# Splitting the later modulation products between GpSimd and ScalarE in a one-core transformer block

## The chip, the cores and the metric

The kernel runs on one core of a Trainium2 chip. The time of an execution is device time in microseconds from its first to its last instruction, with what lies around it. The core has five instruction queues that run side by side and meet through semaphores: TensorE (PE, matmuls; PEld is its loading of weights), VectorE (DVE), ScalarE (ACT), GpSimd (POOL) and SyncE (SP, which here only issues DMAs). Each queue executes strictly in the order in which its instructions were written.

## What is computed

A transformer block on 256 tokens of width 2048, in float32: modulation from a conditioning vector c, one wide projection, a gated delta net (GDN) beside a sparse attention (NSA), a mixing and output projection, and a mixture of 16384 small experts (PEER).

```python
    cs = jax.nn.silu(c)
    for l in range(DEPTH):
        mod = cs @ ada_w[l] + ada_b[l]
        sh1, sc1, g1, sh2, sc2, g2 = [m[:, None, :] for m in jnp.split(mod, 6, axis=-1)]
        h = _rmsnorm(x, norm1_w[l]) * (1.0 + sc1) + sh1
        (a_q, a_k, a_v, a_z, a_a, a_b, b_q, b_kc, b_vc, b_ks, b_vs, b_kw, b_vw, b_g,
         m_a, m_b) = jnp.split(h @ w_in[l], offsets, axis=-1)
        o_a = _gated_deltanet(a_q, a_k, a_v, a_z, a_a, a_b, gdn_conv_w[l], gdn_A_log[l],
                              gdn_dt_bias[l], gdn_norm_w[l])
        o_b = _nsa(b_q, b_kc, b_vc, b_ks, b_vs, b_kw, b_vw, b_g, positions,
                   cmp_pos_k[l], cmp_w1_k[l], cmp_w2_k[l], cmp_pos_v[l], cmp_w1_v[l], cmp_w2_v[l])
        y = jax.nn.sigmoid(m_a) * (o_a @ w_branch_gdn[l]) + jax.nn.sigmoid(m_b) * (o_b @ w_branch_nsa[l])
        x = x + g1 * (y @ w_out[l])
        h2 = _rmsnorm(x, norm2_w[l]) * (1.0 + sc2) + sh2
        x = x + g2 * _peer(h2, peer_wq[l], peer_keys1[l], peer_keys2[l], peer_u[l], peer_v[l])
    return _rmsnorm(x, final_norm_w)
```

The first two parts of the modulation (sh1, sc1) are needed at once. The change is about the next three, g1, sh2 and sc2: 3 x 2048 sums of 2048 products with c, needed only when `w_out` is done.

## The kernel before

**Weights.** Every dense weight passes through one stream (`Stream`). SyncE loads raw tiles of 128x1024 (512 KB, `raw`), into four slots after the first stage. Each half is split into a high part by ScalarE (`whi`, `S.copy`) and the rest by VectorE (`wlo`, raw minus whi); five such pairs can lie ready (`NSPL = 5`). TensorE makes six matmuls of 128x512 from one pair. A raw slot is loaded anew when the pair's `wlo` is done.

**Stages.** Up to about 205 us the first projections run with the modulation's first parts; then the rest of the wide projection with the GDN heads beside it (tiles qkv, cv, kb, vb, XY, N, o); then attention (P, PT, obh); then the two branch projections (`wn`, in four units of 16 weight slices, each ended by `sb<-ps,sb` and `sb<-sa,sb` on VectorE) and `wo` (again four units, each ended by `x<-ps,g1b`, `x<-x,xr`, a square with a row sum on ScalarE and a store `x1d<-x` by GpSimd). From about 1045 us on the experts run to the end.

**Background work.** Dense units are written out one after the other. Between their matmuls a planner (`Background`, with a table of costs in `Times`) steps small tasks whose times have come, so the order of all queues is settled when the program is built. When its clock has advanced by `PACE` (4.5) or, after the last GDN head, `PACE2` (3.3), it also takes one step of `ada_gen`.

**Later modulation.** `ada_gen` is `ada_late((G1, SH2, SC2), ...)`. A step takes one 128x512 tile of the weights (`adas`, two buffers, loaded by SyncE from `ada_t`), multiplies it by a copy of c (`crow`) and sums each row into one column of `acol`, all in one VectorE instruction (SCALAR_TENSOR_TENSOR and its read of the accumulator). Then it issues the load of the tile after next into the slot that has come free. 64 steps make one part; the sums go to `mcol`, and g1 also through `adarow` to `modr`, from where it is loaded as `g1b`. A second use of `ada_late`, for g2 in the experts' stage, has its own tiles.

**The keys' tiles.** `kv_rot` (for kc, ks and kw) and `vcvs_task` (for vc) copy projected keys and values from PSUM to `kv_t`, two tiles a call from one pool of three buffers. Keys are rotated on VectorE, then all are transposed by TensorE.

**GpSimd's queue** in this part of the program holds clears (`o`, `PTc`) and DMA issues: `mix<-partd` and `mix<-mixd` (partial results that a dense unit will use), `sa`, `sb`, `g1b`, `xr` and the stores `x1d`.

Of the kernel before, what the change touches and what calls it, by code (L numbers as in the profile page):

```python
# [7 lines left out]
F32 = mybir.dt.float32  # L8
# [4 lines left out]
AF = mybir.ActivationFunctionType  # L13
OP = mybir.AluOpType
# [145 lines left out]
def flat(ap, off, *dims):  # L160
    return bass.AP(tensor=ap.tensor, offset=ap.offset + off, ap=[list(x) for x in dims])
# [229 lines left out]
def build(nc, tc, A, out, dump=None, stop=None):  # L391

    dump = dump or (lambda n, a: None)

    def at(name):
        if stop == name:
            raise Stop()

    stacks = []
    with ExitStack() as top:  # L400
        top.enter_context(tc.manual_schedule())
        try:
            _build(nc, tc, A, out, stacks, dump, at, stop)
        except Stop:
            pass
        for s in reversed(stacks):
            s.close()


def _build(nc, tc, A, out, stacks, dump, at, stop_at):  # L410
    times = Times()
    V, S, G, PE, SP = (Timed(e, n, times) for e, n in (
        (nc.vector, "V"), (nc.scalar, "S"), (nc.gpsimd, "G"), (nc.tensor, "P"), (nc.sync, "Q")))
# [5 lines left out]
    def pool(st, name, bufs=1, space=None, side=None):  # L419
        kw = {}  # L420
        if space is not None:
            kw["space"] = space
        if side is not None:
            kw["side"] = side
        return TimedPool(st.enter_context(tc.tile_pool(name=name, bufs=bufs, reuse_waits="tile", **kw)), name, bufs, times)
# [7 lines left out]
    def ps():  # L433
        return pss.tile([128, 512], F32, name="ps")

    def act(out, in_, func, bias=0.0, scale=1.0, **kw):
        return S.activation(out, in_, func, bias=bias, scale=scale, **kw)
# [10 lines left out]
    def wait_for(what):  # L448
        while what not in done:
            yield  # L450
# [196 lines left out]
    sbp = pool(st_a, "adasb", side=LEFT)  # L647
    n2T = sbp.tile([128, KT], F32, name="n2T")
    crow = sbp.tile([128, D], F32, name="crow")
# [65 lines left out]
                          start=True, stop=True)  # L715
            V.tensor_copy(dst[:, k4 * 512:(k4 + 1) * 512], p)

    def ada_late(parts, crow, acol, row, room):

        raws = []  # L720
        n = 64 * len(parts)

        def load():
            m = len(raws)
            r = room(m)
            SP.dma_start(r, flat(A["ada_t"], (64 * (parts[m // 64] - 2) + m % 64) * 128 * 512, (512, 128), (1, 512)))
            raws.append(r)

        for _ in range(2):
            load()  # L730
        yield
        for i, part in enumerate(parts):
            for m in range(64):
                r = raws[64 * i + m]
                q = m % 4
                V.scalar_tensor_tensor(r, r, 1.0, crow(q), op0=OP.mult, op1=OP.mult,
                                       accum_out=acol[:, m // 4, q:q + 1])
                if len(raws) < n:
                    load()
                yield  # L740
            col = mcol[:, part, :]
            V.tensor_reduce(col, acol, axis=AX.X, op=OP.add)
            V.tensor_tensor(col, col, adabT[:, 16 * part:16 * part + 16], OP.add)
            if part == SC2:
                V.scalar_tensor_tensor(col, col, 1.0, n2T, op0=OP.add, op1=OP.mult)
            if part in (G1, G2):
                yield bg.now() + 4.0
                p = ps()
                PE.transpose(p[:16, 0:128], col, ident)
                S.copy(row, p[:16, 0:128])  # L750
                G.dma_start(flat(modr, D if part == G2 else 0, (128, 16), (1, 128)), row)
            done.add(part)
            yield

    ada_gen = ada_late((G1, SH2, SC2), lambda q: crow[:, 512 * q:512 * q + 512], sbp.tile([128, 16, 4], F32, name="acol"),
                       sbp.tile([16, 128], F32, name="adarow"),
                       lambda m: sbp.tile([128, 512], F32, name="adas", bufs=2))

    def ada_until(*parts):

# [124 lines left out]
    rp = pool(st_f, "rp", side=LEFT)  # L885
# [124 lines left out]
    def rope(dst, src, tb, n):  # L1010

        t1 = rp.tile([128, n, 32], F32, name="rt1", bufs=2)
        b = lambda a, s: a[:, tb, None, s].to_broadcast([128, n, 16])
        lo, hi = slice(0, 16), slice(16, 32)
        V.tensor_tensor(t1[:, :, lo], src[:, :, hi], b(rs, lo), OP.mult)
        V.tensor_tensor(t1[:, :, hi], src[:, :, lo], b(rs, hi), OP.mult)
        V.tensor_tensor(dst[:, :, 0:32], src[:, :, 0:32], rc[:, tb, None, :].to_broadcast([128, n, 32]), OP.mult)
        V.tensor_tensor(dst[:, :, 0:32], dst[:, :, 0:32], t1, OP.add)

    def transpose_to(p, src, n):  # L1020
        for i in range(n):
            PE.transpose(p[:, i * 128:(i + 1) * 128], src[:, i, :], ident)
        return p[:, :n * 128].rearrange("p (n t) -> p n t", n=n)

    def kv_rot(a, o, dst, free):

        rts = []
        for tb in range(2):
            r = rp.tile([128, 2, 128], F32, name="kv_t", bufs=3)
            S.copy(r, a[tb][:, o:o + 256].rearrange("p (g d) -> p g d", g=2))  # L1030
            rts.append(r)
        banks.give(free)
        yield from wait_for("rope")
        yield
        for tb in range(2):
            rope(rts[tb], rts[tb], tb, 2)
        yield
        yield from banks.take()
        p = ps()
        for tb in range(2):  # L1040
            transpose_to(p[:, tb * 256:(tb + 1) * 256], rts[tb], 2)
        yield
        V.tensor_copy(dst.rearrange("p g (b t) -> p b g t", b=2), p.rearrange("p (b g t) -> p b g t", b=2, g=2))
        banks.give()
# [224 lines left out]
    def kc_task():  # L1269
        yield from kv_rot(c0, 64, kcT[:, 0], 1)  # L1270
        done.add("kc")
# [7 lines left out]
    def vcvs_task(a):  # L1279
        vt = []  # L1280
        for tb in range(2):
            r = rp.tile([128, 2, 128], F32, name="kv_t", bufs=3)
            S.copy(r, a[tb][:, 0:256].rearrange("p (g d) -> p g d", g=2))
            V.tensor_copy(vsw[:, tb, 0], a[tb][:, 256:512].rearrange("p (g d) -> p g d", g=2))
            vt.append(r)
        banks.give(2)
        yield
        p = ps()
        for tb in range(2):
            transpose_to(p[:, tb * 256:(tb + 1) * 256], vt[tb], 2)  # L1290
        S.copy(kcT[:, 1].rearrange("p g (b t) -> p b g t", b=2), p.rearrange("p (b g t) -> p b g t", b=2, g=2))
        yield from wait_for("kc")
        yield
        windows(0)
        yield
        windows(1)
        done.add("vc")

    def kskw_task(a):
        for w in range(2):  # L1300
            yield from kv_rot(a, 256 * w, kT[:, :, w, :], 2 * w)
        done.add("k")
# [58 lines left out]
    def windows(i):  # L1361
        lq, w = i // 2, i % 2
        for g in range(2):
            s = kcT[:, w, g, :]
            win = bass.AP(tensor=s.tensor, offset=s.offset + 4 * lq, ap=[list(s.ap[0]), [1, 4], [16, 15]])
            V.tensor_tensor(blocks[i % 3][:, :, g, 0:15], win,
                            cpos[:, w, 4 * lq:4 * lq + 4, None].to_broadcast([128, 4, 15]), OP.add)
# [45 lines left out]
    cmp_gen = cmp_task()  # L1413

    kv_tasks = dict(vcvs=vcvs_task, kskw=kskw_task, vw=vw_task)
    for n in ORDER:
        if n[0] == "m":
# [515 lines left out]
    def g2_task():  # L1933

        crow = [last_load(vp_(), flat(crowd, 1024 * i, (0, 128), (1, 1024))) for i in range(2)]
        room, small = vp_(), vp_()
        x1_load(0)
        start = bg.now()
        for m, v in enumerate(ada_late((G2,), lambda q: crow[q // 2][:, q % 2 * 512:q % 2 * 512 + 512],
                                       small[:, 0:64].rearrange("p (n q) -> p n q", q=4), small[0:16, 128:256],  # L1940
                                       lambda m: room[:, m % 2 * 512:m % 2 * 512 + 512])):
            yield -max(start + G2PACE * m, bg.now() + 2.0, v or 0.0)
        for half in range(2):
            g2b.append(last_load(vp_(), flat(modr, D + 1024 * half, (0, 128), (1, 1024))))
        x1_load(1)
        for half in range(2):
            fwb.append(last_load(vp_(), flat(A["fnw"], 1024 * half, (0, 128), (1, 1024))))
        done.add("last")
# [124 lines left out]
```

## Time and profile before

| | us |
|---|---|
| median of 3 runs | 2617.65 (2614.93 to 2621.04) |
| the profiled execution | 2625.61 |
| its span, first to last instruction | 2623.8 |
| busy: PE, DVE, ACT, POOL | 2561.7, 1873.9, 1416.3, 521.1 |
| later modulation, first to last product | 224.2 to 1036.3 |

Busy shares are averages over the whole span; what an edit in one stage is worth is read from the waits of that stage. All kernel lines appear as L293, the helper that records every operation, so groups are told apart by their tiles. `ps` is a PSUM tile, `ht` one of the activations' tiles.

### The profile page before, as it was taken

Reading aid. Unit: us, or ns where it says so; the run is one execution under the profiler, and the core shown is the slowest. Engines: PE = TensorE matmul, PEld = TensorE weight load, DVE = VectorE, ACT = ScalarE, POOL = GpSimd, SP = SyncE. Lnnn points to the kernel's source line nnn. Section 1 sums busy time; section 2 is a strip of 40 time slices with the busy share of each in tenths; the row PEclk is TensorE's granted clock in tenths of the full one; section 3 lists DMA queues with packets and bytes.
Section 4 is the critical chain, followed back from the end, with each engine's and each line's share of the span. In section 5 each row is a group of like instructions: output and inputs, shape, how many; then the busy total and the mean of one; then the engine's idle time right before and its main releaser. Section 6 shows DMA issues by size and latency. Waiting matters only on the chain.

```text
span 2623.8 us, 42855 instructions
## 1 busy us (share of the span) xinstructions
PE 2561.7 (98%) x14774; PEld 2122.5 (81%) x14774; DVE 1873.9 (71%) x4089; ACT 1416.3 (54%) x2901; POOL 521.1 (20%) x467
## 2 busy tenths in 40 slices
PE   7999999999999999999999999999999999999998
PEld 5777777686877777999998888888778888888886
DVE  5666877776778776889885555555588887766666
ACT  3435756655555444555555555555555555655555
POOL 0001000000000000016666666662011112000000
PEclk9999999999999999999999999999999999999999
DMA  8887866667676887456666776776588888555554
GB/s 329 333 306 271 277 220 222 236 239 254 216 253 225 287 289 260 179 179 184 183 183 186 189 185 185 189 186 200 212 297 292 288 292 295 189 187 191 185 190 155
DMA packets 229130, 604.60 MB, mean 230 GB/s; under 512 B 59984, under 2 KB 60320, under 8 KB 228400
## 3 DMA queue, kind: packets, MB, share of 16 engines
q1 hardware_dynamic: 168336, 538.21, 58.7%
q0 software_dynamic: 49632, 40.58, 8.9%
q10 hardware_dynamic: 10944, 23.07, 2.3%
q8 instruction: 116, 1.90, 0.3%
q14 instruction: 102, 0.84, 0.1%
HBM read 571.72 MB, written 30.04 MB: 229 GB/s over the span
## 4 chain that ended last, share of the span: by engine, by line
PE 85%; DVE 6%; DMA 4%; ACT 3%; issue 1%; ACTq 0%; DVEq 0%; SPq 0%; POOLq 0%
PE ps L293 85%; DVE wlo L293 2%; DMA adas<-ada_t 2%; DMA raw<-w_in 1%; ACT whi L293 1%; DMA ht<-ada_t 1%; DVE adas L293 1%; DVE cv L293 1%; ACT L293 0%; ACT o L293 0%; DVE A L293 0%; DVE ht L293 0%; DMA ccom<-consts 0%; ACT gsq L293 0%; DVE big L293 0%
## 5 line engine op out<-in xcount | busy, mean ns | idle before, releaser
L293 DVE TENSOR_TENSOR wlo<-raw,whi 128x512 fp32r<-128x512 f32 (+2 forms) x1632 | 1099.6, 685 | 526.0 <-ACT whi L293 494.7
L293 ACT CAST whi<-raw 128x512 fp32r<-128x512 f32 (+2 forms) x1632 | 997.3, 617 | 770.3 <-PE ps L293 615.7
L293 PE MATMUL ps<-ht,whi 128*128 128x256 f32 (+1 forms) x3152 | 817.6, 335 | 0.8 <-DVE ht L293 0.8
L293 PE MATMUL ps<-ht,wlo 128*128 128x256 f32 x2304 | 648.5, 281 | 0.3
L293 PEld LDWEIGHTS ps<-ht,whi 128*128 128x128 f32 x3152 | 533.5, 188 | 68.7 <-DVE ht L293 1.0
L293 PE MATMUL ps<-whi,ht 128*128 128x512 f32 (+2 forms) x1536 | 522.4, 402 | 8.2 <-ACT whi L293 4.0
L1851 POOL DMA_INDIRECT gated<-gate,place x256 | 416.1, 1625 | 294.8 <-DMA gated<-gate,place 177.0
L293 PEld LDWEIGHTS ps<-ht,wlo 128*128 128x128 f32 x2304 | 434.2, 188 | 1.0 <-DVE wlo L293 0.9
L293 PE MATMUL ps<-wlo,wh 128*128 128x512 f32 x1024 | 407.2, 398 | 4.1 <-DVE wlo L293 4.1
L293 PE MATMUL ps<-whi,wl 128*128 128x512 f32 x1024 | 406.7, 397 | 0.0
L293 PE MATMUL ps<-whi,wh 128*128 128x512 f32 x1024 | 403.8, 394 | 2.0 <-ACT wh L293 2.0
L293 PEld LDWEIGHTS ps<-whi,ht 128*128 128x128 f32 x1536 | 289.5, 190 | 92.1 <-issue 12.4
L293 PE MATMUL ps<-wlo,ht 128*128 128x512 f32 (+2 forms) x768 | 300.8, 392 | 6.3 <-DVE wlo L293 6.1
L293 PEld LDWEIGHTS ps<-wlo,wh 128*128 128x128 f32 x1024 | 193.0, 189 | 52.9 <-DVE wlo L293 5.4
L293 PEld LDWEIGHTS ps<-whi,wh 128*128 128x128 f32 x1024 | 192.8, 188 | 50.3 <-ACT wh L293 2.3
L293 PEld LDWEIGHTS ps<-whi,wl 128*128 128x128 f32 x1024 | 193.1, 189 | 45.2 <-DVE wl L293 0.2
L293 ACT CAST wh<-A 128x256 fp32r<-128x256 f32 x256 | 103.9, 407 | 135.8 <-PE ps L293 130.3
L293 PEld LDWEIGHTS ps<-wlo,ht 128*128 128x128 f32 x768 | 146.5, 191 | 35.0 <-DVE wlo L293 10.8
L293 DVE SCALAR_TENSOR_TENSOR adas<-adas,crow 128x512 f32<-128x512 f32 x192 | 131.4, 685 | 36.7 <-DMA adas<-ada_t 36.3
L293 DVE TENSOR_TENSOR wl<-A,wh 128x256 fp32r<-128x256 f32 x256 | 108.7, 425 | 48.8 <-ACT wh L293 48.1
L293 POOL DMA_DIRECT2D gates<-gated x128 | 68.4, 539 | 353.5 <-DVE A L293 340.7
L293 ACT COPY aj<-ps 128x256 f32<-128x256 f32 x91 | 33.9, 373 | 78.6 <-PE ps L293 78.6
(319 smaller groups left out, 2204.6 us busy)
## 6 DMA issues: line engine op xcount, KB each, us to landing
raw<-u SPq DMA_DIRECT2D x256, 512.0 KB, 3.6
raw<-v SPq DMA_DIRECT2D x256, 512.0 KB, 4.2
raw<-w_in SPq DMA_DIRECT2D x170, 512.0 KB, 4.9
adas<-ada_t SPq DMA_DIRECT2D x192, 256.0 KB, 3.7
raw<-ada_w SPq DMA_DIRECT2D x64, 512.0 KB, 6.7
gated<-zero ACTq DMA_DIRECT2D x64, 256.0 KB, 4.1
raw<-wn SPq DMA_DIRECT2D x32, 512.0 KB, 4.7
raw<-wo SPq DMA_DIRECT2D x32, 512.0 KB, 5.0
```

Source lines behind the costliest of these rows:

```text
L293: r = f(*args, **kw)
L1851: nc.gpsimd.indirect_dma_start(gated[tb].rearrange("i j (t o) -> (i j t) o", o=1), bass.IndirectOffsetOnAxis(ap=place[:, tb, n:n + 1], axi ...
```

## The change

`ada_late` gets a parameter, `pool`. Where it is set, as for `ada_gen`, a step is two instructions: GpSimd multiplies the tile by c in place, and ScalarE copies the tile onto itself with a row sum into `acol`. The loads, the two `adas` buffers and the pace stay. The pool of `kv_t` gets a fourth buffer. The use for g2 is not changed.

```diff
@@ -715,7 +715,7 @@
-    def ada_late(parts, crow, acol, row, room):
+    def ada_late(parts, crow, acol, row, room, pool=False):
@@ -733,8 +733,12 @@
                 r = raws[64 * i + m]
                 q = m % 4
-                V.scalar_tensor_tensor(r, r, 1.0, crow(q), op0=OP.mult, op1=OP.mult,
-                                       accum_out=acol[:, m // 4, q:q + 1])
+                if pool:
+                    G.tensor_tensor(r, r, crow(q), OP.mult)
+                    act(r, r, AF.Copy, accum_out=acol[:, m // 4, q:q + 1])
+                else:
+                    V.scalar_tensor_tensor(r, r, 1.0, crow(q), op0=OP.mult, op1=OP.mult,
+                                           accum_out=acol[:, m // 4, q:q + 1])
                 if len(raws) < n:
                     load()
                 yield
@@ -754,7 +758,7 @@
-                       lambda m: sbp.tile([128, 512], F32, name="adas", bufs=2))
+                       lambda m: sbp.tile([128, 512], F32, name="adas", bufs=2), True)
@@ -1026,7 +1030,7 @@
-            r = rp.tile([128, 2, 128], F32, name="kv_t", bufs=3)
+            r = rp.tile([128, 2, 128], F32, name="kv_t", bufs=4)
@@ -1279,7 +1283,7 @@
-            r = rp.tile([128, 2, 128], F32, name="kv_t", bufs=3)
+            r = rp.tile([128, 2, 128], F32, name="kv_t", bufs=4)
```

Since the planner counts GpSimd's and ScalarE's time otherwise than VectorE's, the whole order after about 205 us is laid anew. Two places show what stands where.

ScalarE at the second unit of `wn`, around the first cast to `yh` (the transposed result of the first unit), in the kernel before:

```order
L293 CAST whi_9666<-raw_9553 128x512
L293 CAST whi_9679<-raw_9553 128x512
L293 CAST whi_9691<-raw_9578 128x512
L293 CAST yh_9643<-ps_9698 128x4x128
L293 CAST whi_9716<-raw_9578 128x512
L293 CAST yh_9643<-ps_9708 128x4x128
```

and now:

```order
L293 CAST whi_9831<-raw_9719 128x512
L293 ACTIVATE adas_9748,acol_107<-adas_9748 128x512
L293 CAST whi_9845<-raw_9719 128x512
L293 CAST whi_9857<-raw_9741 128x512
L293 CAST whi_9867<-raw_9741 128x512
L293 ACTIVATE adas_9777,acol_107<-adas_9777 128x512
L293 CAST whi_9883<-raw_9767 128x512
L293 ACTIVATE adas_9843,acol_107<-adas_9843 128x512
L293 CAST yh_9808<-ps_9890 128x4x128
```

A row sum of adas stands between the casts to whi, after every one to three of them, and each waits for its product on GpSimd.

GpSimd where the branch projections' inputs are loaded (`sa`, `sb`, two buffers each), in the kernel before:

```order
L293 DMA mix_9075<-mixd_2200 128x1024
L293 DMA sa_9648<-mixd_2200 128x1024
L293 DMA sb_9649<-mixd_2200 128x1024
L293 DMA sa_9652<-mixd_2200 128x1024
L293 DMA sb_9653<-mixd_2200 128x1024
L293 DMA sa_9660<-mixd_2200 128x1024
L293 DMA sb_9661<-mixd_2200 128x1024
```

and now:

```order
L293 TENSOR_TENSOR adas_9713<-adas_9713,crow_96 128x512
L293 DMA sa_9813<-mixd_2200 128x1024
L293 DMA sb_9814<-mixd_2200 128x1024
L293 DMA sa_9817<-mixd_2200 128x1024
L293 DMA sb_9818<-mixd_2200 128x1024
L293 DMA sa_9825<-mixd_2200 128x1024
L293 DMA sb_9826<-mixd_2200 128x1024
L293 TENSOR_TENSOR adas_9748<-adas_9748,crow_96 128x512
L293 TENSOR_TENSOR adas_9777<-adas_9777,crow_96 128x512
```

The products of adas stand behind loads that wait for a buffer (the third `sa` for the first one's use), here and at the loads of mix and the stores of x1d.

## Rows read from the trace of the kernel before

**Rows 1.** The page's head: span, and each engine's busy time.

```profile
span 2623.8 us, 42855 instructions
PE 2561.7 (98%) x14774; PEld 2122.5 (81%) x14774; DVE 1873.9 (71%) x4089; ACT 1416.3 (54%) x2901; POOL 521.1 (20%) x467
```

**Rows 2.** The tile adas: duration (min/median/max, ns), first and last start; landing.

```profile
L293 DVE SCALAR_TENSOR_TENSOR adas<-adas,crow x192: 669/684/694, 224.2 to 1036.3; 128x512 f32<-128x512 f32 x192
...
DMA to landing us min/median/max: 2.4/3.7/8.9
```

**Rows 3.** Stretches (us from the start): each engine's busy time, clock, DMA.

```profile
core 0: us, PE busy (x) PEld busy (x) DVE busy (x) ACT busy (x) POOL busy (x), PEclk, DMA share, GB/s
205.00:300.00 95.00, 92.71 (x485) 72.33 (x484) 69.14 (x187) 64.67 (x142) 7.76 (x23) 1.00 0.79 271
205.00:1045.00 840.00, 811.50 (x4802) 637.96 (x4801) 629.34 (x1641) 473.52 (x1107) 24.41 (x57) 0.99 0.73 250
```

**Rows 4.** TensorE's waits, 205 to 1045 us: total, times, longest.

```profile
PE ps L293 <- DVE wlo L293: 11.6, 17, 3.4
PE ps L293 <- ACT whi L293: 3.1, 4, 1.3
PE ps L293 <- DVE XY L293: 2.4, 2, 1.8
PE ps L293 <- ACT N L293: 2.2, 2, 2.0
PE ps L293 <- DVE cv L293: 2.2, 2, 1.6
PE ps L293 <- DVE mix L293: 2.1, 3, 1.2
```

**Rows 5.** VectorE's waits, 205 to 1045 us: the one for adas.

```profile
DVE adas L293 <- DMA adas<-ada_t: 36.3, 20, 5.0
```

**Rows 6.** Five stretches around VectorE's longest waits for adas: the first, the sum.

```profile
604.90:614.30 9.40, 6.00 (x26) 4.50 (x24) 4.14 (x10) 3.00 (x5) 0.00 (x0) 0.93 0.83 290
...
sum 44.00, PE 35.72 PEld 27.13 DVE 20.93 ACT 17.99 POOL 0.18; mean PE 7.14 PEld 5.43 DVE 4.19 ACT 3.60 POOL 0.04
```

**Rows 7.** Groups by form, 205 to 1045 us: busy us, mean ns | idle before.

```profile
L293 DVE TENSOR_TENSOR wlo<-raw,whi 128x512 fp32r<-128x512 f32 x427 | 285.6, 688 | 128.4 <-ACT whi L293 125.3
L293 ACT CAST whi<-raw 128x512 fp32r<-128x512 f32 x426 | 257.5, 623 | 227.2 <-PE ps L293 164.1 <-DMA raw<-w_in 20.0 <-DVE mx L293 14.3
...
L293 DVE SCALAR_TENSOR_TENSOR adas<-adas,crow 128x512 f32<-128x512 f32 x192 | 131.4, 685 | 36.7 <-DMA adas<-ada_t 36.3
...
L293 DVE DVE_READ_ACCUMULATOR adas<-adas,crow 128x1 f32 x192 | 15.7, 82 | 0.0
```

**Rows 8.** The same view: ScalarE's square with a row sum, and its read.

```profile
L293 ACT ACTIVATE ps<-x 128x512 f32<-128x512 f32 x6 | 3.6, 602 | 11.5 <-DVE x L293 11.5
...
L293 ACT ACTIVATION_READ_ACCUMULATOR ps<-x 128x1 f32 x6 | 1.1, 187 | 0.0
```

**Rows 9.** ScalarE's waits: whi from 205 to 1045 us, kv_t before 300 us.

```profile
ACT whi L293 <- PE ps L293: 168.0, 207, 4.8
...
ACT kv_t L293 <- PE ps L293: 3.0, 1, 3.0
```

**Rows 10.** SyncE's own waits, 205 to 1045 us.

```profile
SPq L293 <- DVE adas L293: 316.1, 180, 6.1
```

**Rows 11.** GpSimd's groups by form: clears.

```profile
L293 POOL MEMSET PTc<- 128x256 f32 x3 | 0.8, 331 | 0.0
...
L293 POOL MEMSET blocks<- 128x8 f32 x3 | 0.2, 131 | 0.0
```

**Rows 12.** Timelines: ScalarE's store of mix, GpSimd's loads; [idle before <-releaser].

```profile
599.74 0.33 ACTq L293 DMA_DIRECT2D mixd<-mix  x1
...
603.82 0.53 POOL L293 DMA_DIRECT2D mix<-mixd  x1 [9.81 <-ACT oah L293]
...
889.01 0.53 POOL L293 DMA_DIRECT2D sa<-mixd  x1 [14.83 <-DVE sb L293]
```

## The prediction

> **What bounds the kernel now.** I read the page's head first, then the stretches, the waits of TensorE, and last the tile that the change touches. TensorE is busy 98% of a span of 2623.8 us [rows 1]: whatever happens on other engines counts only where it makes TensorE wait. The edited steps run from 224.2 to 1036.3 us [rows 2], so one stretch matters, 205 to 1045 us. TensorE is busy 811.5 of its 840 us there [rows 3]: 28.5 us of idle time is all that any edit of VectorE's work can win. VectorE is busy 629.3 us there (75%), ScalarE 473.5 us (56%), GpSimd 24.4 us.
>
> Who makes TensorE wait: the rows that name VectorE are 11.6, 2.4, 2.2 and 2.1 us, with small ones some 20 us; those that name ScalarE are 3.1 and 2.2 us, with small ones some 7 us [rows 4]. VectorE itself stands still 36.3 us, in 20 places, the longest 5.0 us, for the arrival of an adas tile (a slice of the modulation's weights) [rows 5], which lands 3.7 us after its issue in the median and 8.9 us at worst [rows 2]. In the five places where that stall is longest, TensorE is busy 35.7 of 44.0 us [rows 6]: 8.3 us lost. So 8.3 of 36.3 us, 0.23, is the share of such a stall that reaches TensorE; the split weights that lie ready (five whi/wlo pairs) hide the rest.
>
> **Part 1, what is taken from VectorE.** 192 products of 0.685 us and 192 accumulator reads of 0.082 us [rows 7] are 147 us; VectorE falls from 629 to 482 us of 840 (57%). On the path of this: the 8.3 us of the five places go, since VectorE no longer waits for adas. Of the other 12 us that name VectorE I take half, because much of it is a single result awaited (XY, cv, kd), not a long queue. Together **-14 us**; ends 0 and -20.
>
> **Part 2, what ScalarE gets.** 192 copies of a 128x512 tile with a row sum. The nearest row is the square with a row sum of the same size, 0.602 us and its read 0.187 us [rows 8]; a 128x512 cast from SBUF is 0.623 us [rows 7]. So 0.79 to 0.81 us each, 151 to 156 us, 156 taken: ScalarE rises from 473.5 to 630 us, 75%, which is just what VectorE had. It has 168 us in which its next cast only waits for a free buffer [rows 9], so on average the work fits; but the casts to whi, at the head of every weight's way to TensorE, now stand behind it. I price this by symmetry: at 75% VectorE cost 20 us less the 8.3 of its DMA stalls, ScalarE at 56% costs 7. Difference **+5 us**; ends 0 and +13.
>
> **Part 3, the row sum waits for the product.** ScalarE executes in order; its row sum waits for GpSimd's product, which waits for the tile. What is queued behind the waiting row sum is the next cast to whi, and wlo and TensorE behind that. SyncE's queue waits too: it reuses the adas slot only after the row sum, and it already stands 316 us in all for the release of adas with weight loads behind it [rows 10]. A product of two SBUF tiles on GpSimd is in no row. From below: clearing 128x256 takes 0.331 us and 128x8 0.131 us [rows 11], 0.8 ns a column, so writing 512 columns is 0.54 us. From above: two reads and one write at that rate, 1.3 us, an estimate from these rows; it is also about twice VectorE's 0.685 us. I take 1.3.
>
> Beside this, the Trainium skill (GPSIMD Engine Reference, Performance versus the Vector engine) gives 4.5 us for such an operation on 2048 columns; a quarter is an estimate of 1.1 us, and no row here shows it. With that the term below would be some 1 us smaller.
>
> The 192 tiles come 812/191 = 4.25 us apart and two are in flight, so a slot turns over in 8.5 us, of which the product and its read took 0.8 and the landing takes 3.7: 4 us to spare on average, and 20 tiles were late all the same. Now 1.3 us of this goes. The 20 late ones wait 1.8 + 1.3 = 3.1 us each (62 us); I add 15 newly late ones at half a product (10 us). ScalarE then waits 72 us where VectorE waited 36. At the share of 0.23: **+16 us**. Ends: 0, if ScalarE always arrives later than the product, and 24, at the share of the five worst places alone (8.3 us of at most five times 5.0 us, 0.33).
>
> **Part 4, GpSimd's queue.** The products share a queue that in before held DMA issues and clears with nothing pressing behind them. In the built order products stand behind loads of mix, behind sa and sb, behind clears of o and behind stores of x1d, about 13 places. Such a load waits: for mix until the store of the old tile is through, which on the trace is 4.1 us after that store's issue (issue 599.74, load 603.82), and for sa until VectorE has used the old one, 14.8 us of standing [rows 12]. The product, 1.3 us, comes after that and after the 0.53 us of the issue, some 6 us after the store; ScalarE's next row sum is due 4.25 us after it. About 2 us a place, 26 us, at 0.23: **+6 us**, ends 0 and 9. The loads of mix, sa and xr themselves are pushed back by a product or two, at 1.3 us; they are issued a whole unit of 16 weight slices ahead, and that covers it.
>
> **Parts that cost nothing.** The fourth buffer for kv_t: in before one copy to kv_t stood 3.0 us for its buffer, beside TensorE busy 92.7 of 95 us [rows 3, 9]; in the built order all eight transposes of kc and vc stand together, and the fourth buffer makes that possible. Taken at 0, ends -1 and +1. TensorE's instructions are the same in number, only interleaved otherwise. Table loads on ScalarE do not grow (one fewer in the build). An instruction ahead of GpSimd's first product is new; GpSimd has next to nothing to do until then and waits for the tile anyway, so 0, ends 0 and +2.
>
> **Sum:** -14 + 5 + 16 + 6 = +13 us. The profiled execution took 2625.6 us (span 2623.8 us and 1.8 around it), 8 us above the median 2617.65 us of the runs shown; the sum makes 2639 against the one and 2631 against the other. I give 2631.
>
> **The rivals.**
> *Relief wins.* ScalarE fits the row sums into its 168 us of slack and the products are always ready: then only part 1 counts, -14 us, **2604 us**. For it: GpSimd is idle 97% of the stretch, and tiles have 4 us to spare on average. Against: late tiles are already 20 of 192, and the new chain is longer. It decides by whether ScalarE's wait for the products stays under some 36 us. Chance 0.27.
> *Nothing moves.* The gain of part 1 and the costs cancel, within 5 us of the median, **2618 us**. For it: TensorE idles only 3.4% of the stretch. Chance 0.18.
> *The two engines block each other.* VectorE's difference wlo reads two SBUF tiles (raw and whi), and it is 285.6 of VectorE's 629 us [rows 7]; GpSimd's product reads two as well. If a wlo that meets a product stands until it is over, 192 products of 1.3 us hold VectorE up by at most 250 us; by half of that VectorE is back at 607 us, where it was, and part 1 is void: 5 + 16 + 6 = +27 us, **2645 us**. Nothing in this trace shows or excludes it, since GpSimd only clears and issues DMAs in the stretch. It decides if wlo's mean, 0.688 us, rises to about 0.98 us (125 us over its 427 instructions). Chance 0.20.
> The Trainium skill (SBUF — State Buffer, Who interferes with whom) states this as a rule: a VectorE instruction with two SBUF inputs contends with a GpSimd instruction that reads SBUF, and the later one is held until the first is done. By that rule the time is that rival's, 2645 us; by the present rows alone it would be 2631 us.
>
> **How the numbers follow.** My forecast, the sum, has 0.35, the blocking 0.20, no change 0.18, relief 0.27. A measurement of this kernel can tell about 0.2%, 5 us. So slower 0.55, same 0.18, faster 0.27. The ends of all parts together are -20 and about +46 us (13 + 24 + 9); the range from 2603 to 2657 us takes in relief's 2604 and the blocking's 2645 with some 10 us for its own spread, and leaves out a tenth on each side. The forecast's own range is 2622 to 2640.
>
> **What the changed profile would show.** Part 1: VectorE near 480 us between 205 and 1045 us and no wait of VectorE for adas. Part 2: ScalarE near 630 us, a row sum at 0.60 and a read at 0.19 us. Part 3: a row "ScalarE adas waits for GpSimd adas" of 70 to 100 us; under 36 us speaks for relief. Part 4: GpSimd's adas waiting behind mix, sa and x1d. The blocking: wlo far over 0.69 us wherever GpSimd runs a product. TensorE's idle time of the stretch should be some 41 us instead of 28.5. I am wrong if products take 3 us or more (row sums then wait everywhere), or if TensorE's idle time falls below 20 us.

## The result and the profile after

The changed kernel takes 2701.15 us in the median of 4 runs (2693.60 to 2703.15), the kernel before 2619.07 us beside it (2614.93 to 2621.04). The ratio is 1.0318, 95% interval 1.0299 to 1.0336: some 83 us slower, where 13 us were forecast and the range ended at 2657 us. The profiled execution took 2699.98 us, its span 2698.2 us.

The page's head of after; it answers to [rows 1]:

```profile
span 2698.2 us, 43145 instructions
PE 2585.5 (96%) x14774; PEld 2127.4 (79%) x14774; DVE 1850.3 (69%) x3705; ACT 1522.4 (56%) x3284; POOL 793.9 (29%) x659
...
PE 72%; DVE 9%; DMA 6%; ACT 6%; issue 4%; POOL 2%; ACTq 0%; SPq 0%; DVEq 0%; POOLq 0%
```

The last line is the page's chain that ended last. VectorE is hardly less busy than it was (1850.3 against 1873.9 us), although 192 instructions of 0.685 us and their reads have left it.

Stretches of after: microseconds, busy time of each engine (instructions), TensorE's granted clock, DMA share, GB/s. The last row holds all the edited steps (the last product starts at 1075.8 us, before at 1036.3) and ends where TensorE has done about as much as before by 1045 us [rows 3]:

```profile
400.00:500.00 100.00, 86.12 (x482) 64.95 (x481) 72.97 (x163) 70.97 (x175) 23.69 (x19) 0.95 0.67 233
500.00:800.00 300.00, 281.48 (x1758) 220.22 (x1758) 200.85 (x440) 198.56 (x528) 101.12 (x83) 1.00 0.69 233
...
900.00:1000.00 100.00, 82.48 (x333) 62.44 (x333) 52.99 (x79) 47.35 (x112) 41.16 (x36) 0.91 0.70 233
...
205.00:1125.00 920.00, 840.63 (x4823) 647.68 (x4822) 608.19 (x1260) 579.73 (x1491) 288.26 (x249) 0.97 0.68 229
```

The same work of TensorE (4823 matmul records, 4802 before) takes 920 us instead of 840. TensorE's idle time there is 79.4 us, where it was 28.5, and its busy time is 840.6 us, where it was 811.5. Much of the second part, 29 us, goes with the clock: over the stretch the granted clock is 0.97 of 2.4 GHz, where it was 0.99. By these rounded figures that is an estimate of some 19 us (0.03 of 920 less 0.01 of 840); what the rest is, the rows don't tell. It is lowest, 0.91, in the hundred microseconds in which TensorE stands still most, 17.5 us. Between 930 and 940 us it is 0.58, near the lower of its two levels, 1.2 GHz, after ten microseconds in which TensorE was busy 6.55 of 10:

```profile
920.00:930.00 10.00, 6.55 (x29) 4.91 (x27) 4.70 (x8) 1.48 (x3) 1.38 (x4) 1.00 1.02 385
930.00:940.00 10.00, 6.42 (x20) 4.57 (x21) 2.68 (x5) 3.41 (x8) 4.58 (x5) 0.58 0.62 205
```

Groups of after by form, 205 to 1125 us (busy us, mean ns, idle before and its releasers), which answer to [rows 7, 8]:

```profile
L293 DVE TENSOR_TENSOR wlo<-raw,whi 128x512 fp32r<-128x512 f32 x428 | 346.7, 839 | 247.7 <-ACT whi L293 245.9
L293 POOL TENSOR_TENSOR adas<-adas,crow 128x512 f32<-128x512 f32 x192 | 263.9, 1378 | 532.8 <-DMA adas<-ada_t 386.0 <-ACT whi L293 69.9 <-ACT adas L293 24.4
L293 ACT ACTIVATE adas<-adas 128x512 f32<-128x512 f32 x192 | 122.0, 635 | 154.9 <-POOL adas L293 147.8 <-DVE sm L293 4.7 <-DVE mcol L293 1.6
L293 ACT ACTIVATION_READ_ACCUMULATOR adas<-adas 128x1 f32 x192 | 37.2, 194 | 0.0
```

Two things stand in these rows. VectorE's wlo takes 839 ns in the mean, where it took 688, though nothing of it was edited. By the trace's start and end times, the 146 of the 428 that overlap a product of GpSimd take 1136 ns in the mean, and the other 282 take 686, as before. And ScalarE's row sum waits 147.8 us for GpSimd's products. The waits of after (total us, times, longest), of ScalarE, TensorE and SyncE's queue, answer to [rows 4, 9, 10]:

```profile
ACT adas L293 <- POOL adas L293: 147.8, 78, 13.6
ACT whi L293 <- PE ps L293: 56.3, 73, 4.5
```

```profile
PE ps L293 <- ACT whi L293: 25.4, 15, 7.3
PE ps L293 <- DVE wlo L293: 24.8, 32, 3.6
```

```profile
SPq L293 <- DVE wlo L293: 357.3, 170, 13.6
SPq L293 <- ACT adas L293: 266.6, 103, 13.9
```

TensorE waits for both halves of the split weights now. ScalarE's slack, the time in which a cast waited for a free buffer, fell from 168.0 to 56.3 us: the casts are late, where they used to be early. SyncE's queue stands no longer for the release of adas than before (266.6 against 316.1 us).

The chain that ended last, from 970 us on (start, us, what), shows one round of the loop:

```profile
971.93 0.73 ACT adas L293 x2
972.65 0.02 issue
972.67 5.42 DMA adas<-ada_t
...
978.22 1.31 POOL adas L293
...
980.10 0.19 ACT adas L293
980.28 0.52 ACT whi L293
980.80 0.02 issue
980.82 1.03 DVE wlo L293
```

A row sum ends, its slot is loaded again (5.42 us), GpSimd multiplies (1.31 us), ScalarE sums, and only then comes the cast to whi that stood behind the sum, and wlo behind the cast. A wlo of 1.03 us ends the piece.

### The profile page after: what moved, and what is told of

It is laid out like the page before. It is cut to its first block, busy times and chain, and to the rows that moved or that the text cites. A ratio compares the mean times of both kernels' runs of the same rounds, so it can differ in the third digit from the quotient of the medians.

```text
span 2698.2 us, 43145 instructions
## 1 busy us (share of the span) xinstructions
PE 2585.5 (96%) x14774; PEld 2127.4 (79%) x14774; DVE 1850.3 (69%) x3705; ACT 1522.4 (56%) x3284; POOL 793.9 (29%) x659
## 4 chain that ended last, share of the span: by engine, by line
PE 72%; DVE 9%; DMA 6%; ACT 6%; issue 4%; POOL 2%; ACTq 0%; SPq 0%; DVEq 0%; POOLq 0%
PE ps L293 72%; DMA adas<-ada_t 5%; DVE wlo L293 4%; ACT whi L293 2%; POOL adas L293 2%; ACT adas L293 1%; ACT L293 1%; DMA raw<-w_in 1%; DVE A L293 1%; DVE cv L293 1%; ACT P L293 1%; DMA ht<-ada_t 1%; ACT gsq L293 0%; DVE P L293 0%; ACT o L293 0%
## 5 line engine op out<-in xcount | busy, mean ns | idle before, releaser
L293 DVE TENSOR_TENSOR wlo<-raw,whi 128x512 fp32r<-128x512 f32 (+2 forms) x1632 | 1161.1, 726 | 639.9 <-ACT whi L293 579.5
L1855 POOL DMA_INDIRECT gated<-gate,place x256 | 424.9, 1660 | 286.0 <-DMA gated<-gate,place 169.5
L293 POOL TENSOR_TENSOR adas<-adas,crow 128x512 f32<-128x512 f32 x192 | 263.9, 1378 | 532.8 <-DMA adas<-ada_t 386.0
L293 ACT ACTIVATE adas<-adas 128x512 f32<-128x512 f32 x192 | 122.0, 635 | 154.9 <-POOL adas L293 147.8
```

What stands on the lines that cost most here:

```text
L293: r = f(*args, **kw)
L1855: nc.gpsimd.indirect_dma_start(gated[tb].rearrange("i j (t o) -> (i j t) o", o=1), bass.IndirectOffsetOnAxis(ap=place[:, tb, n:n + 1], axi ...
```

## The experiments

Three theories stood at the start. **Wait**: the loop of load, product and row sum through two tiles makes ScalarE late, and the casts behind it. **Port**: GpSimd's product and VectorE's instructions hold each other up. **Order**: the planner's new order of work is worse by itself. A fourth, **occupancy**, is that ScalarE merely has more to do. Times below stand against runs of the kernel before on the same chip, 2616 us in each of the three sets.

### The order alone, and the split alone

In the first kernel the planner reckons with the two new instructions, so that the order is the changed kernel's, but VectorE's old instruction does the work:

```diff
-                    G.tensor_tensor(r, r, crow(q), OP.mult)
-                    act(r, r, AF.Copy, accum_out=acol[:, m // 4, q:q + 1])
+                    times.note("G", "tensor_tensor", (r, r, crow(q), OP.mult), {})
+                    times.note("S", "activation", (r, r, AF.Copy), dict(bias=0.0, scale=1.0, accum_out=acol[:, m // 4, q:q + 1]))
+                    V.engine.scalar_tensor_tensor(r, r, 1.0, crow(q), op0=OP.mult, op1=OP.mult,
+                                                  accum_out=acol[:, m // 4, q:q + 1])
```

> The changed kernel's order of work, as its planner set it with the costs of the two new instructions, but at each of the 192 steps VectorE's single instruction (product with row sum) as before; four kv_t buffers. If the new order is what costs the time (theory order): 2680 us or more. If the waits of the two-engine step (theory wait) or the block between GpSimd and VectorE (theory port) cost it: 2620 +- 12 us, wlo's mean at about 0.69 us as before and no wait of ScalarE's row sum, since there is none.

2620.55 us, ratio 1.0015 [1.0000, 1.0030]. The second is the reverse: the planner reckons with VectorE's instruction, and the two new ones do the work.

```diff
-                    G.tensor_tensor(r, r, crow(q), OP.mult)
-                    act(r, r, AF.Copy, accum_out=acol[:, m // 4, q:q + 1])
+                    times.note("V", "scalar_tensor_tensor", (r, r, 1.0, crow(q)), dict(op0=OP.mult, op1=OP.mult, accum_out=acol[:, m // 4, q:q + 1]))
+                    G.engine.tensor_tensor(r, r, crow(q), OP.mult)
+                    S.engine.activation(r, r, AF.Copy, bias=0.0, scale=1.0, accum_out=acol[:, m // 4, q:q + 1])
```

> The reverse: the order of work of the kernel before, as its planner set it with VectorE's cost, but at each of the 192 steps the product on GpSimd and the row sum on ScalarE; four kv_t buffers. Theory order: 2620 us. Theories wait and port: 2690 to 2710 us, wlo's mean at about 0.84 us, ScalarE waiting about 150 us for the products.

2693.48 us, ratio 1.0299 [1.0271, 1.0327]: nearly the whole loss. The order, with the fourth kv_t buffer that both these kernels have, costs some 4 us (0 to 8); theory order falls.

### A third tile

The changed kernel with three adas tiles. Their room comes from a smaller tile of zeros and from `gsq` in bfloat16; what these two change by themselves was not measured.

```diff
-        zero = per.tile([128, 512], F32, name="zero")
+        zero = per.tile([128, 128], F32, name="zero")
...
-                S.dma_start(g[:, js:js + 4].rearrange("i j t -> i (j t)"), zero)
+                S.dma_start(g[:, js:js + 4].rearrange("i (a b) t -> i a (b t)", a=4), zero[:, None, :].to_broadcast([128, 4, 128]))
...
-        for _ in range(2):
+        for _ in range(ahead):
...
-                       lambda m: sbp.tile([128, 512], F32, name="adas", bufs=2), True)
+                       lambda m: sbp.tile([128, 512], F32, name="adas", bufs=3), True, 3)
...
-    gsq = pg.tile([128, 128], F32, name="gsq")
+    gsq = pg.tile([128, 128], BF, name="gsq")
```

> The changed kernel with three adas tiles and three loads ahead of the step in place of two (the room comes from a smaller tile of zeros, read repeatedly by its DMAs, and from gsq in bfloat16). Theory wait: a load has one step more to land before its product is due, so most of ScalarE's 148 us of waiting for products goes and the time comes back to 2640 to 2655 us. Theory port: GpSimd runs the same 192 products beside VectorE, so wlo's mean stays at about 0.84 us and the time at 2685 to 2700 us.

2657.49 us, ratio 1.0152 [1.0120, 1.0185]. It lies just above what theory wait expected (2640 to 2655 us), and below what theory port did. ScalarE's wait for products, and wlo by form, 205 to 1125 us:

```profile
ACT adas L293 <- POOL adas L293: 37.7, 19, 6.6
```

```profile
L293 DVE TENSOR_TENSOR wlo<-raw,whi 128x512 fp32r<-128x512 f32 x450 | 378.3, 867 | 190.9 <-ACT whi L293 188.4 <-DMA raw<-wn 0.7
```

The wait fell from 147.8 to 37.7 us and half of the loss went with it. The other half stayed, and wlo stayed slow. Neither theory alone is enough.

### A product that reads nothing

The changed kernel with the product left out; two clears of the same tile stand in its place.

```diff
-                    G.tensor_tensor(r, r, crow(q), OP.mult)
+                    G.memset(r, 0.0)
+                    G.engine.memset(r, 0.0)
```

> The changed kernel with the product of each step left out: two GpSimd memsets of the same tile stand in its place, for about as long (2 x 0.55 us, an estimate from the memsets in the kernel before) but reading nothing; the row sums on ScalarE wait for them as for the product. Part of the modulation is thus not computed. Theory port: wlo's mean back to about 0.69 us and the time at about 2640 us or below. Theory wait: wlo may move but the loop load - GpSimd - row sum stands as before, so 2685 us or more and ScalarE's wait for GpSimd near 148 us.

2661.70 us, ratio 1.0179 [1.0149, 1.0209], between what the two theories expected. By form and among ScalarE's waits, 205 to 1125 us:

```profile
L293 DVE TENSOR_TENSOR wlo<-raw,whi 128x512 fp32r<-128x512 f32 x447 | 295.3, 687 | 303.6 <-ACT whi L293 301.0 <-DMA raw<-w_in 1.4
...
L738 POOL MEMSET adas<- 128x512 f32 x192 | 101.1, 527 | 11.0
```

```profile
ACT adas L293 <- POOL adas L738: 142.4, 74, 14.3
```

GpSimd is occupied for 1.05 us a step instead of 1.38, writes the same tile twice, and wlo is back at 687 ns: what held it up is something that the product does and a clear does not. The plain difference is that the product reads SBUF; that it is this is argued, not shown. The wait is as long as before (142.4 us), and so is the other half of the loss.

### Both cures at once

The third tile and the clears in one kernel, which leaves the product out as well; against the kernel with the third tile:

```diff
-                    G.tensor_tensor(r, r, crow(q), OP.mult)
+                    G.memset(r, 0.0)
+                    G.engine.memset(r, 0.0)
```

> Both cures at once: the changed kernel with two GpSimd memsets in place of each product (the product is left out, so part of the modulation is not computed) and with three adas tiles and three loads ahead. If the loss of the changed kernel is the sum of a block between GpSimd and VectorE, a wait through two tiles and ScalarE's occupancy, each by itself: the first two are gone and only the occupancy stands (the spare row sums cost 16 us), less what VectorE's relief gives back: 2605 to 2632 us. If the two cures took away the same thing twice: about 2650 us.

2614.26 us, ratio 0.9996 [0.9980, 1.0011]: all of the loss is gone. The two causes are different ones and add up. From the ratios, times 2616 us: without the third tile, 1.0179 less 0.9996 is **48 us for the wait**; with the product in place of the clears, 1.0152 less 0.9996 is **41 us for the block**; each within some 10 us by the intervals. -1 + 48 + 41 = 88 us is what the changed kernel should lose if they add, and it loses 83. (The 41 us hold a little more than the block: the product is longer than the two clears, and ScalarE waits 37.7 us for it against 26.7 us here. With two tiles, the changed kernel less the one with clears gives 1.0318 less 1.0179, 36 us.) TensorE's wait for wlo agrees: 24.8 us in the changed kernel, 10.8 with clears; 15.5 with the third tile, 2.5 with both.

### The block alone

The kernel before, where VectorE keeps its instruction, with one GpSimd product more in each step that nobody reads or waits for:

```diff
+                if len(parts) == 3:
+                    G.engine.tensor_tensor(spare, crow(q), crow(q), OP.mult)
...
+    spare = sbp.tile([128, 512], BF, name="spare")
```

> The kernel before, with one GpSimd product more at each of the 192 steps (crow times crow, 128x512 float32 in, bfloat16 out to a spare tile) that nobody reads or waits for; VectorE's instruction stays. Theory port: GpSimd's reads hold VectorE up as in the changed kernel, wlo's mean at about 0.8 us and 40 to 80 us more (2660 to 2700 us). Theory wait: nobody waits for it, so 2618 to 2630 us.

2710.09 us, ratio 1.0380 [1.0345, 1.0414]: work that nobody waits for costs more than the whole change, and more than theory port expected. The mean of wlo is 855 ns, and nothing on VectorE waits for a load of GpSimd's queue. Since nothing paces these products, they run in rows, 46 of the 192 between 205 and 270 us. Two timelines there (start, us, engine, what, how many):

```profile
229.65 20.17 POOL L739 TENSOR_TENSOR spare<-crow 128x512 bf16<-128x512 f32 x15
```

```profile
231.30 1.52 DVE L293 SCALAR_TENSOR_TENSOR adas<-adas,crow 128x512 f32<-128x512 f32 x1
...
232.76 4.40 DVE L293 TENSOR_TENSOR wlo<-raw,whi 128x512 fp32r<-128x512 f32 x3
```

GpSimd's products follow each other every 1.34 us (20.17/15), and three wlo take 4.40 us, 1.47 us each instead of 0.69: each VectorE instruction with two SBUF inputs takes some 0.8 us longer, over half of one product. In that stretch TensorE is busy 45.1 of 65 us and its granted clock is 0.84:

```profile
205.00:270.00 65.00, 45.12 (x153) 32.26 (x151) 56.65 (x72) 23.10 (x43) 61.15 (x67) 0.84 0.44 147
```

Rows of products are not what the changed kernel has. So the next kernel paces them: a small GpSimd copy ahead of each product reads the sum that VectorE has written in that step.

```diff
+                    G.engine.tensor_copy(tok, acol[:, m // 4, q:q + 1])
                     G.engine.tensor_tensor(spare, crow(q), crow(q), OP.mult)
...
-    spare = sbp.tile([128, 512], BF, name="spare")
+    spare, tok = sbp.tile([128, 512], BF, name="spare"), sbp.tile([128, 1], F32, name="tok")
```

> The kernel before with the spare GpSimd product of crow by crow again, but each one held back until VectorE's instruction of its step has written its sum (a 128x1 GpSimd copy reads that sum first), so that the 192 products are spread as the steps are and don't run one behind the other; still nobody waits for them. Theory port: each product stands against VectorE's next instructions, 30 to 60 us more: 2645 to 2680 us, wlo's mean at about 0.78 us. If the 94 us of the unpaced products came from their running in rows alone, for instance through the long stretch at 205 to 270 us: 2616 to 2630 us.

2647.98 us, ratio 1.0135 [1.0107, 1.0163], 35 us. Groups by form, 205 to 1125 us:

```profile
L293 DVE TENSOR_TENSOR wlo<-raw,whi 128x512 fp32r<-128x512 f32 x454 | 335.9, 760 | 108.9 <-ACT whi L293 106.6
L740 POOL TENSOR_TENSOR spare<-crow 128x512 bf16<-128x512 f32 x192 | 226.6, 1180 | 0.2 <-POOL tok L739 0.2
L293 DVE SCALAR_TENSOR_TENSOR adas<-adas,crow 128x512 f32<-128x512 f32 x192 | 151.8, 790 | 13.4 <-DMA adas<-ada_t 13.1
```

In these two groups VectorE is held up (760 - 688) x 454 + (790 - 685) x 192 ns = 53 us, and the kernel loses 35: 0.66 us for each. That is an upper value. Other instructions of VectorE are held up too, and it waits 8.0 us for a load of sb and 8.2 us for one of g1b, which stand behind products in GpSimd's queue; before it waited for neither. With the third tile, wlo is held up (867 - 688) x 450 ns = 81 us, against the block's 41: 0.51. With two tiles it is (839 - 688) x 428 ns = 65 us against 36: 0.56.

### Occupancy, relief and kv_t alone

Three kernels take the smaller terms one by one, each from the kernel before. A row sum more on ScalarE in each step, that waits for nobody:

```diff
+                if len(parts) == 3:
+                    S.engine.activation(spare, crow(q), AF.Copy, bias=0.0, scale=1.0, accum_out=ssum)
...
+    spare, ssum = sbp.tile([128, 512], BF, name="spare"), sbp.tile([128, 1], F32, name="ssum")
```

> The kernel before, with one ScalarE copy with row sum more at each of the 192 steps (of crow, into a spare tile) that reads nothing that another engine makes at that time; VectorE's instruction stays. It puts 192 x about 0.82 us = 157 us of busy time on ScalarE and no wait. If ScalarE's occupancy by itself is what costs the time (theory occupancy): 2660 us or more. Theories wait and port: 2618 to 2632 us.

2631.35 us, ratio 1.0065 [1.0038, 1.0093]: 17 us (10 to 24). Occupancy has a price of its own, far less than the theory of that name wanted; it lies at the upper end of what the other theories left for it. The slack of the casts falls, from 185.3 us between 205 and 1125 us in the kernel before to 122.8:

```profile
ACT whi L293 <- PE ps L293: 122.8, 186, 4.1
```

VectorE's instruction cut to 16 columns (the rest of its sum is left out):

```diff
-                V.scalar_tensor_tensor(r, r, 1.0, crow(q), op0=OP.mult, op1=OP.mult,
-                                       accum_out=acol[:, m // 4, q:q + 1])
+                w = slice(0, 16 if len(parts) == 3 else 512)
+                times.note("V", "scalar_tensor_tensor", (r, r, 1.0, crow(q)), dict(op0=OP.mult, op1=OP.mult, accum_out=acol[:, m // 4, q:q + 1]))
+                V.engine.scalar_tensor_tensor(r[:, w], r[:, w], 1.0, crow(q)[:, w], op0=OP.mult, op1=OP.mult,
+                                              accum_out=acol[:, m // 4, q:q + 1])
```

> The kernel before with VectorE's instruction of each of the 192 steps cut from 128x512 to 128x16 (the rest of its sum is left out, so part of the modulation is not computed), in the same order: the largest relief of VectorE that the change can give, about 115 us of its busy time, with nothing added elsewhere. The prediction's Part 1 took 14 us for the relief: about 2602 us. If VectorE's time is hidden: 2616 +- 4 us.

2601.82 us, ratio 0.9950 [0.9933, 0.9966]: 13 us gained (9 to 18). Each step falls from 685 to 168 ns, and yet VectorE's wait for the loads of adas is still there, 39.5 us in 29 places, so the gain hardly comes from that wait; what is left is VectorE's other work, which comes earlier:

```profile
L738 DVE SCALAR_TENSOR_TENSOR adas<-adas,crow 128x16 f32<-128x16 f32 x192 | 32.2, 168 | 39.6 <-DMA adas<-ada_t 39.5
```

Four kv_t buffers and nothing else:

```diff
-            r = rp.tile([128, 2, 128], F32, name="kv_t", bufs=3)
+            r = rp.tile([128, 2, 128], F32, name="kv_t", bufs=4)
...
-            r = rp.tile([128, 2, 128], F32, name="kv_t", bufs=3)
+            r = rp.tile([128, 2, 128], F32, name="kv_t", bufs=4)
```

> The kernel before with four kv_t buffers in place of three and nothing else. The one wait that three buffers cause is 3.0 us of ScalarE in the whole stretch: 2619 +- 5 us by every theory.

2612.61 us, ratio 0.9984 [0.9964, 1.0003]: no difference that these runs tell.

### A kernel that is faster than both

Three tiles and three loads ahead, but in the kernel before, with VectorE's one instruction:

```diff
-        zero = per.tile([128, 512], F32, name="zero")
+        zero = per.tile([128, 256], F32, name="zero")
...
-                S.dma_start(g[:, js:js + 4].rearrange("i j t -> i (j t)"), zero)
+                S.dma_start(g[:, js:js + 4].rearrange("i (a b) t -> i a (b t)", a=2), zero[:, None, :].to_broadcast([128, 2, 256]))
...
-        for _ in range(2):
+        for _ in range(ahead):
...
-                       lambda m: sbp.tile([128, 512], F32, name="adas", bufs=2))
+                       lambda m: sbp.tile([128, 512], F32, name="adas", bufs=3), ahead=3)
```

> The kernel before, VectorE's single instruction at each step, with three adas tiles and three loads ahead (room from a smaller tile of zeros that its DMAs read repeatedly). VectorE's 36.3 us of waiting for the adas loads should go; what reaches TensorE of it is taken at the share of the prediction, 0.23: 2619 - 8 = 2611 us if the loads' lateness matters to the kernel before (theory wait, its milder form), 2619 +- 5 us if it is hidden.

2605.55 us, ratio 0.9970 [0.9952, 0.9989]. VectorE's wait for adas falls from 36.3 us to

```profile
L293 DVE SCALAR_TENSOR_TENSOR adas<-adas,crow 128x512 f32<-128x512 f32 x192 | 131.3, 684 | 11.2 <-DMA adas<-ada_t 11.1
```

and 8 us are gained (3 to 13); the 25 us that are gone would give 6 at the prediction's share of 0.23. With four kv_t buffers added, whose room comes from a still smaller tile of zeros:

```diff
-        zero = per.tile([128, 256], F32, name="zero")
+        zero = per.tile([128, 64], F32, name="zero")
...
-            r = rp.tile([128, 2, 128], F32, name="kv_t", bufs=3)
+            r = rp.tile([128, 2, 128], F32, name="kv_t", bufs=4)
```

> The kernel before with three adas tiles, three loads ahead and four kv_t buffers together (the tile of zeros cut to 64 columns that its DMAs read repeatedly). If the two gains add, -10.5 us and -3.4 us: 2602 us, against 2606 us with three tiles alone; if the kv_t gain was chance: 2606 us.

2611.34 us, ratio 0.9981 [0.9967, 0.9995]. The gains don't add. Whether the kv_t gain was chance or the smaller reads of the zeros cost it was not told apart.

## Why the prediction was wrong, step by step

The forecast was slower, and it is slower, by six times as much. Two steps failed above all: the price of ScalarE's wait (Part 3, +16 us, measured 48), and the block between GpSimd and VectorE, which stood in the sum at nothing and measured 41. The terms measured singly are relief -13 and -8, occupancy +17, wait +48, block +41, in sum +85 us against +83 measured. The intervals leave some 16 us either way, and the 27 us of ScalarE's wait that a third tile doesn't cure stand in none of the terms, so the closeness is partly luck.

**Part 1, relief (-14, ends 0 and -20).** Its two halves were measured apart. The wait for adas was to give 8.3 us, and the third tile in the kernel before, which takes 25 of its 36 us, gives 8. VectorE's other work was to give 6, and the cut instruction, in whose kernel the wait stands (39.5 us), gives 13. So the relief was taken rather too small. What failed is the mark that I set for it, VectorE near 480 us: it is busy 608. Even with clears, where wlo is not held up, it is busy 514 us while TensorE does the same work (205 to 1085 us there, 4798 matmul records). The 147 us were a sum of durations that overlap their neighbours, so some 115 us of busy time left VectorE, and the rest up to 608 us is wlo and others held up.

**Part 2, occupancy (+5, ends 0 and +13).** The durations were right: 0.635 + 0.194 = 0.83 us a step against 0.81 forecast. The price was too small: 17 us. The step that failed is the symmetry with VectorE. The likely reason is argued, not shown: ScalarE stands at the head of each weight's way, and a row sum ahead of a cast delays the cast, the wlo and the matmul behind it. But TensorE's own waits for whi and wlo are together no longer with the spare row sums (3.6 and 9.8 us) than before (3.1 and 11.6).

**Part 3, the row sum's wait (+16, ends 0 and 24).** The mechanism is the one of the text, and the product's 1.30 us in the median is what it took (1.3). Both other factors were too small. ScalarE waits 147.8 us at 78 places, where I had 72 us at 35: I counted the 20 tiles late before and 15 new ones from an average spacing of 4.25 us, but the steps and the landings are not even, and a late row sum also makes the next load late, as the chain shows. And 48 us for the 116 us of wait that the third tile takes away in the kernels with clears (142.4 less 26.7) is 0.41 for each us, not 0.23, and more than the 0.33 of the range's end. That share was the idle time of five stretches set against all of VectorE's stalls, 20 in 812 us; 78 stalls of an engine one step further ahead leave the split weights less time to pile up again. That the density is the reason is argued, not shown.

**Part 4, GpSimd's queue (+6).** Seen but not measured by itself: in the chain, between 960 and 969 us, the product stands behind the loads of sa and sb, of which the first waits for VectorE. The runs with clears keep this queue, so what it costs ScalarE lies within the wait's 48 us.

```profile
960.56 4.87 issue
965.43 0.04 POOLq L293
965.47 0.56 POOL sa L293
966.03 2.35 issue
968.38 0.02 POOLq L293
968.40 0.10 POOL sb L293
968.50 0.46 issue
968.96 1.29 POOL adas L293
```

What the prediction held to be covered, the loads pushed back by products, was not quite: VectorE waits 5.1 us for sb, 3.3 for g1b, 2.8 for xr and 1.4 for mix, where it waited for none of them before, and with the new order alone only 1.2 us, for mix. What TensorE loses by that was not measured.

**kv_t and the order (0).** Right within what can be told: -4 us [-9, +1] and +4 us [0, +8].

**The rival of the block (2645 us, chance 0.20).** This is the step that failed most. It was set up as one case among four, with a chance of 0.20, and so stood in the forecast's sum at nothing, though by its own terms it comes on top of the waits. Its price was wrong too: I voided Part 1 with it, 14 us for 125 us of VectorE's time, as though being held up only made VectorE as busy as it had been. But wlo itself, the last step before a matmul, comes out later, and TensorE waits for it (24.8 us against 10.8 with clears). Of wlo less time was held up than the rival had (839 ns in the mean, not 980: 65 us; VectorE's other instructions bring some 27 more by the trace), and each microsecond of it cost 0.5 to 0.6, not 0.11.

The Trainium skill (SBUF — State Buffer, Who interferes with whom) has the rule that was cited there as a sentence beside the rival. The traces agree with it in both halves: a VectorE instruction with two SBUF inputs is held up by a GpSimd instruction that reads SBUF (839 ns), and not by one that only writes (687 ns beside 384 clears).

The other rivals, relief and no change, fall: the wait that was to decide, "under some 36 us", is 147.8 us.

The clock is part of every term: in the stretch with the most idle time of TensorE its granted clock fell furthest, and busy time rose by 29 us with hardly any more matmuls in the trace, some 19 of it by the clock (the estimate above). The prediction took idle time alone (from 28.5 to some 41 us; it is 79.4) and had no term for the clock.

## What to carry to other kernels

Before work is moved to GpSimd, list VectorE's instructions that read two SBUF operands on the critical way: here GpSimd's products held them up, though no semaphore joins the two, and the price went with the delay of wlo, not with VectorE's share of busy time. When one engine's step becomes a chain through two in-order engines, give the tile a buffer more in the same edit, and put the chain's end on an engine that nothing urgent stands behind (the buffer was tried here, the other engine was not). Costs that come from different mechanisms add up; a list of rivals that exclude each other hides that.

## What the runs showed of the hardware

By these rows, where the operands lie goes with what is held up. By form, after, 205 to 1125 us:

```profile
L293 DVE TENSOR_TENSOR XY<-XY,ps 128x256 f32<-128x256 f32 x32 | 12.4, 416 | 1.0 <-PE ps L293 0.7
...
L293 DVE TENSOR_TENSOR sb<-sa,sb 128x512 f32<-128x512 f32 x8 | 7.0, 880 | 0.3
L293 DVE TENSOR_TENSOR sb<-ps,sb 128x512 f32<-128x512 f32 x8 | 5.5, 683 | 5.1 <-DMA sb<-mixd 5.1
```

The sum of two SBUF tiles takes 880 ns (692 before), and the same sum with one operand in PSUM 683, as before. In the kernel with clears both are as in the kernel before, but a third kind is not, an instruction with one tile, in SBUF, as its input (`sm` is a column):

```profile
L293 DVE TENSOR_SCALAR P<-P,sm 128x128 f32<-128x128 f32 x32 | 9.0, 356 | 0.6
L293 DVE TENSOR_TENSOR sb<-sa,sb 128x512 f32<-128x512 f32 x8 | 5.5, 692 | 0.3
L293 DVE TENSOR_TENSOR sb<-ps,sb 128x512 f32<-128x512 f32 x8 | 5.5, 683 | 4.4 <-DMA sb<-mixd 4.4
```

P took 284 ns in the kernel before:

```profile
L293 DVE TENSOR_SCALAR P<-P,sm 128x128 f32<-128x128 f32 x32 | 7.7, 284 | 0.6
```

In the kernel with clears, the 15 that overlap a clear take 438 ns in the mean and the other 17 take 284. So clears do hold up something, only not wlo. The Trainium skill (SBUF — State Buffer, Who interferes with whom) says that VectorE's tensor_scalar can run in a mode that takes the pair of ports it shares with GpSimd; 284 against 356 ns agrees with that.

In a row of spare products without a gap, products and VectorE's instructions with two SBUF inputs come at nearly the same pace, 1.34 and 1.47 us. And 384 clears of 128x512 at 0.53 us do not lengthen VectorE's wlo, while the 192 products of the changed kernel lengthen it by 65 us in all.
